# Layer-norm DMAs moved from ScalarE's queue to GpSimd's, with other buffers, copy priorities and filler positions at the end of a dilated attention

## Chip, cores and metric

One core of one Trainium2 chip. The metric is the device time of one execution in microseconds (us), the median of the runs shown. Engines: PE (TensorE), with PEld its weight loads, DVE (VectorE), ACT (ScalarE), POOL (GpSimd) and SP (SyncE, which here only issues DMAs). A name with q (ACTq, SPq) is an engine's instruction queue.

## What is computed

Two encoder layers on x of 512 tokens by 1024 features, all in float32. Each has three sub-layers, and each sub-layer ends in a layer norm over 1024 features:

```
x = layer_norm(ALPHA * x + h, ln_g[i, 0], ln_b[i, 0])                                  # h: token mixer
x = layer_norm(ALPHA * x + memory_cross_attention(...), ln_g[i, 1], ln_b[i, 1])
x = layer_norm(ALPHA * x + conv_glu(...), ln_g[i, 2], ln_b[i, 2])
```

The mixer of layer 0 is a differential attention with 8 heads. The mixer of layer 1 is a dilated window attention: 16 heads, three groups of (window, dilation), each with its own projections, merged by their softmax denominators.

## The kernel before

A float32 product is made of three PE passes over float32r halves (`mm3`, L239): high by high, high by low, low by high. Every weight is fetched from DRAM by SP as a 128x1024 tile `raw` (4 buffers) and split into `whi` (a cast on ACT, L219) and `wlo` (a subtraction on DVE, L220). So ACT and DVE feed PE, and DVE's subtraction frees the buffer into which SP fetches next.

**Order of the work.** PE's order is written by hand (`manual_schedule`): `weave` runs a main generator and, at each position that it yields, runs filler matmuls up to a matching share. The order of DVE, ACT, POOL and SP is made by the scheduler from the program's order and priorities; `tc.high_priority(offset=URGENT)` moves an instruction ahead. Each engine then runs its own list strictly in order, so an instruction that waits holds up all behind it, a DMA issue too.

**The dilated attention** (`dil_attention`) has 16 steps, a step being a pair of heads p and a half v of the queries. `scores(p, v)` puts four score tiles S into PSUM (4 buffers); for each, DVE adds the bias and takes the row extreme into a tile `u` (L730), and ACT takes the exponential in place (L732). `u` has 4 buffers, so the four tiles of a step can only be written once the four of the step before have been read. One step later `turn` transposes each of them on PE (L775) into one of two PSUM banks `ps_t`, and a copy to SBUF, `PT`, is made by DVE for tiles 0 and 2 and by ACT for 1 and 3 (L777). `values` (L790) multiplies by the value tiles; its result takes the same two banks. After v = 1 the two partial results `O` are scaled by `F` (L800 to L802) and split into the input of the output projection, `o1h` and `o1l`. `F` comes through `factors` (L745 to L769): small DMAs issued by POOL to DRAM and back.

The fillers are the projections of the next pair of heads and, for the last steps, `on_.early(0)`: the output projection of query block 0, as far as it goes without the last heads. `late` is the same for block 1 (12 units of one `mm3`, 648 by the planner's cost); `take(late, t)` runs units of it until their costs exceed t. In the last step (i = n = 16) there are no scores left: 3 units run at its head, 3 before `values`, the rest after the loop.

**The end of a sub-layer** (`OutNorm.finish`, L357) opens a pool of rows in memory that the attention has left (or in tiles of the ConvGLU). It loads gamma and beta broadcast to 128 partitions (`gb`, L368) and the four residual blocks (`xs`, L373), 512 KB each, by ACT's queue. While PE works through the four query blocks, `norm` (L418) does for each: two accumulating adds on DVE (L422, from PSUM), the mean (L425), the square on ACT (L426), two products (L429), a power -0.5 on POOL (L431), two more products (L434), and after each of the latter a 256 KB DMA of half the block to DRAM (L435), by ACT's queue. `turn` transposes the rows on PE for the next sub-layer (L440). Between, PE runs `mem_keys` (after a mixer): key projections of the memory tokens into two PSUM banks, which ACT and DVE empty into `kv` (L219, L220).

Of the kernel before, what the change touches and what calls it, by code (L numbers as in the profile page):

```python
# [9 lines left out]
F32 = mybir.dt.float32  # L10
# [6 lines left out]
D = 1024  # L17
# [131 lines left out]
def encoder(ctx: ExitStack, tc: tile.TileContext, wall, xin, lam, subln, conv, lngb, tabf, tabd, eye, out):  # L149
# [101 lines left out]
    def sl(k, n=128):  # L251
        return slice(k * n, k * n + n)
# [28 lines left out]
    def take(gen, t):  # L281
        while t > 0:
            d = next(gen, None)
            if d is None:
                break
            t -= d
# [40 lines left out]
    class OutNorm:  # L327
# [29 lines left out]
        def finish(self, banks, first, res, last, turns, lead_in, rows=None, then=(), norm=NORM):  # L357

            ln, nu = self.ln, self.nk // 2
            with ExitStack() as c:
                if rows is None:
                    tp = c.enter_context(tc.tile_pool(name=f"tail{ln}", bufs=1, reuse_waits="tile"))
                    rows = lambda n, dt=F32: tp.tile([128, D], dt, name=f"row{n}")
                gb = [rows(n) for n in range(2)]
                for n in range(2):
                    nc.scalar.dma_start(gb[n], bass.AP(lngb.tensor, lngb.offset + (ln * 2 + n) * D,  # L368
                                                       [[0, 128], [1, D]]))
                xs = [rows(2 + q) for q in range(4)]  # L370
                tmp, sq = rows(6), rows(7, BF16)
                for q in range(4):
                    nc.scalar.dma_start(xs[q], res[sl(q), :])  # L373
                ynext, act = None, None
                if not last:
                    ynext = dram.tile([SEQ, D], F32, name=f"y{ln}")
                    act = new_act(f"x{ln}")

                def left(u, q, hf):
                    if (u, q, hf) not in self.done:  # L380
                        run(self.part(u, q, hf))

                look["n"] = 0
                for us, qs in first:
                    for u in us:
                        self.load(*u)
                    for q in qs:
                        if q not in self.acc:
                            self.acc[q] = banks(q)
                    for u in us:  # L390
                        for q in qs:
                            left(u[0], q, u[1])
                ready = 0.0
                for q in range(4):
                    for us, qs in then if q == 2 else ():
                        for n in qs:
                            for u in us:
                                self.load(*u)
                                left(u[0], n, u[1])
                        pump(len(queue) + 1)  # L400
                    for n, hf in ((q, 0), (1, 0), (q, 1)) if q == 0 else ((q, 0), (q, 1)):
                        for u in range(nu):
                            self.load(u, hf)
                            left(u, n, hf)
                    self.norm(q, xs[q], gb, out if last else ynext, tmp, sq)
                    pump(PUMP[q])
                    if not last:
                        ready = max(ready, pe["now"]) + norm
                        for n in range(2):
                            due.append((ready + 700 * n,  # L410
                                        lambda q=q, n=n, x=xs[q], where=places(turns(q)):
                                        self.turn(q, n, x, act, where(n))))
                look["n"] = LOOK
                led = lead_in(act)
                flush()
                return act, ynext, led

        def norm(self, q, xs, gb, dst, tmp, sq):  # L418
            sm = st.tile([128, 6], F32, name="sm6", tag="sm6")
            for hf in range(2):  # L420
                f = sl(hf, 512)
                nc.vector.scalar_tensor_tensor(xs[:, f], xs[:, f], ALPHA, self.acc[q][hf],  # L422
                                               op0=ALU.mult, op1=ALU.add, accum_out=sm[:, hf:hf + 1])
            nmu, ss, ve, rs = (sm[:, n:n + 1] for n in range(2, 6))
            nc.vector.tensor_scalar(nmu, sm[:, 0:1], sm[:, 1:2], -1.0 / D, op0=ALU.add, op1=ALU.mult)  # L425
            nc.scalar.activation(sq, xs, AF.Square, bias=nmu, accum_out=ss)  # L426
            for n in range(2):
                f = sl(n, 512)
                nc.vector.scalar_tensor_tensor(tmp[:, f], xs[:, f], nmu, gb[0][:, f], op0=ALU.add, op1=ALU.mult)  # L429
            nc.vector.tensor_scalar(ve, ss, 1.0 / D, EPS, op0=ALU.mult, op1=ALU.add)  # L430
            nc.gpsimd.tensor_tensor(rs, ve, mhalf[:, 0:1], op=ALU.pow)  # L431
            for n in range(2):
                f = sl(n, 512)
                nc.vector.scalar_tensor_tensor(xs[:, f], tmp[:, f], rs, gb[1][:, f], op0=ALU.mult, op1=ALU.add)  # L434
                nc.scalar.dma_start(dst[sl(q), f], xs[:, f])  # L435

        def turn(self, q, n, xs, act, ps):
            tps = ps.rearrange("p (a b) -> p a b", b=128)
# [212 lines left out]
    def dil_attention(act, oT, pools, vp, ap, on_, led):  # L651
# [57 lines left out]
        def scores(p, v):  # L709
            (q0, k0, q1, k1, q2, k2) = qk[p]  # L710
            if v == 0:
                st0[p] = ap.tile([128, 4, 4], F32, tag="st0", name="st0")
                st12[p] = ap.tile([128, 4, 4], F32, tag="st12", name="st12")
            bs = 2 * v, 2 * v + 1
            Ss = {(b, c): psS.tile([128, 512], F32, tag="s", name="S") for b in bs for c in range(2)}
            for b in bs:
                for q_, k_, f in ((q0, keys(k0, b), slice(0, 256)), (q1, k1[:, b, :], slice(256, 384)),
                                  (q2, k2[:, b, :], slice(384, 512))):
                    for c in range(2):
                        h = sl(c, 64)  # L720
                        nc.tensor.matmul(Ss[b, c][:, f], q_[h, b, :], k_[h], start=True, stop=True)  # L721
            us = []
            for (b, c), S in Ss.items():
                u = ap.tile([128, 512], F32, tag="u", name="u", bufs=4)
                slope = 2.0 ** (-(2 * p + c + 1) / 2.0)
                for n, s in enumerate((st0[p], st12[p])):
                    f = sl(n, 256)
                    t = tab[:, 512:768] if n else tab[:, sl(b // 3, 256)]
                    m = s[:, b, 2 * c:2 * c + 1]
                    nc.vector.tensor_tensor_reduce(out=u[:, f], in0=S[:, f], in1=t, scale=-slope,  # L730
                                                   scalar=3.0e38, op0=ALU.add, op1=ALU.min, accum_out=m)
                    nc.scalar.activation(u[:, f], u[:, f], AF.Exp, bias=m, scale=-1.0,  # L732
                                         accum_out=s[:, b, 2 * c + 1:2 * c + 2])
                us.append(u)
            if v == 1:
                O[p] = [ap.tile([128, 512], F32, tag=f"O{n}", name="O", bufs=1) for n in range(2)], factors(p)
            return us
# [34 lines left out]
        def turn(u, n):  # L772
            tp = bank(pt, "t").rearrange("p (a b) -> p a b", b=128)
            for k in range(4):
                nc.tensor.transpose(tp[:, k, :], u[:, sl(k)], ident)  # L775
            PT = ap.tile([128, 4, 128], F32, tag="PT", name="PT", bufs=4)
            (nc.scalar.copy if n % 2 else nc.vector.tensor_copy)(PT, tp)  # L777
            return PT

        def values(p, v, PTs):  # L780
# [29 lines left out]
        def main():  # L810
            n = 2 * NP
            us = {}
            for i in range(n + 1):
                seg, step = (i // 2, 1 / 2.0) if i < n - 2 else (NP - 1, 1 / 3.0)
                pos = seg + (i - 2 * seg) * step
                yield pos
                if i < n:
                    us[i] = scores(i // 2, i % 2)
                else:
                    take(late, 1300)  # L820
                if i > 0:
                    PTs = []
                    for k in range(4):
                        yield pos + TURNS[k] * step
                        PTs.append(turn(us[i - 1][k], k))
                    yield pos + VALUES * step
                    if i == n:
                        take(late, 1300)
                    values((i - 1) // 2, (i - 1) % 2, PTs)
# [238 lines left out]
```

## Time and profile before

| | us |
|---|---|
| median of 3 runs | 1895.67 |
| the 3 runs | 1895.67, 1891.98, 1896.01 |
| the profiled execution, its own time | 1891.74 |
| span of its trace, first to last instruction | 1889.9 |
| PE busy in the span | 1864.7 |
| mean granted clock of PE | 0.997 |

The span leaves out 1.84 us of the execution. PE is busy for nearly all of it, so what can be saved without taking matmuls away is the little time in which PE waits, and the time in which it runs at a lower clock.

### The profile page before, as it was taken

The numbers are of one execution on the slowest core, as the hardware profiler recorded it, in microseconds if no ns is written. First come the engines' busy times: TensorE is split into PE (matmuls) and PEld (weight loads), VectorE is DVE, ScalarE is ACT, GpSimd is POOL, SyncE is SP. The second block draws the span as 40 slices with busy tenths as digits, with TensorE's granted clock in tenths as the row PEclk, the third lists the DMA queues.
The fourth block names the chain that finished last, engine by engine and source line by source line (L and its number), as shares of the span: only waits on it lengthen the run. The fifth ranks groups of instructions, "written<-read, shape, count | busy, mean of one in ns | idle before, by whom it ended". The sixth has DMA issues, their size and how long they took to land.

```text
span 1889.9 us, 25002 instructions
## 1 busy us (share of the span) xinstructions
PE 1864.7 (99%) x9896; PEld 1575.4 (83%) x9896; DVE 951.2 (50%) x1761; ACT 762.7 (40%) x1372; POOL 79.7 (4%) x116
## 2 busy tenths in 40 slices
PE   9999989999999999999999999999999999999998
PEld 7777778889888888899898898987888898888886
DVE  5678675547444432443444344445845564444324
ACT  5577644425333321234434344344544343333211
POOL 0011110000000000000000000001100000000000
PEclk9999999999999999999999999999999999999999
DMA  6121165234333234343223232231752343233241
GB/s 238 49 75 45 35 223 187 70 112 157 91 100 100 91 99 144 103 141 101 91 68 94 86 92 88 71 98 47 253 170 67 112 157 100 91 100 100 90 144 45
DMA packets 61573, 204.35 MB, mean 108 GB/s; under 512 B 8080, under 2 KB 8720, under 8 KB 61456
## 3 DMA queue, kind: packets, MB, share of 16 engines
q1 hardware_dynamic: 46080, 165.89, 27.6%
q10 hardware_dynamic: 12816, 32.47, 4.7%
q0 software_dynamic: 2560, 4.39, 1.0%
q8 instruction: 78, 1.28, 0.3%
q14 instruction: 39, 0.32, 0.1%
HBM read 190.01 MB, written 12.71 MB: 107 GB/s over the span
## 4 chain that ended last, share of the span: by engine, by line
PE 89%; DVE 4%; ACT 2%; DMA 2%; issue 1%; POOL 1%; DVEq 0%; POOLq 0%; SPq 0%; ACTq 0%
PE ps_a L240 16%; PE ps_a L241 16%; PE ps_a L242 16%; PE ps_o L240 7%; PE ps_o L241 7%; PE ps_o L242 7%; PE ps_s L242 2%; PE ps_s L241 2%; PE ps_s L240 2%; PE ps_t L240 2%; PE ps_t L242 2%; PE ps_t L241 2%; PE S L721 2%; PE ps_t L790 2%; PE ps_t L775 1%; ACT u L571 1%
## 5 line engine op out<-in xcount | busy, mean ns | idle before, releaser
L220 DVE TENSOR_TENSOR wlo<-raw,whi 128x1024 fp32r<-128x1024 f32 (+1 forms) x309 | 377.0, 1220 | 480.8 <-ACT whi L219 476.2
L219 ACT CAST whi<-raw 128x1024 fp32r<-128x1024 f32 (+1 forms) x309 | 323.9, 1049 | 583.7 <-PE ps_a L241 266.5
L240 PE MATMUL ps_a<-x2h,whi 128*128 128x512 f32 (+1 forms) x384 | 149.3, 389 | 0.0
L242 PE MATMUL ps_a<-x2h,wlo 128*128 128x512 f32 (+1 forms) x384 | 146.5, 382 | 0.0
L241 PE MATMUL ps_a<-x2l,whi 128*128 128x512 f32 (+1 forms) x384 | 146.3, 381 | 0.0
L240 PE MATMUL ps_a<-whi,x2h 128*128 128x512 f32 (+1 forms) x256 | 88.8, 347 | 0.0
L241 PE MATMUL ps_a<-wlo,x2h 128*128 128x512 f32 (+1 forms) x256 | 87.2, 341 | 0.0
L242 PE MATMUL ps_a<-whi,x2l 128*128 128x512 f32 (+1 forms) x256 | 87.2, 341 | 0.0
L242 PEld LDWEIGHTS ps_a<-x2h,wlo 128*128 128x128 f32 x384 | 72.2, 188 | 14.1
L240 PEld LDWEIGHTS ps_a<-x2h,whi 128*128 128x128 f32 x384 | 72.3, 188 | 13.9
L241 PEld LDWEIGHTS ps_a<-x2l,whi 128*128 128x128 f32 x384 | 72.3, 188 | 12.8
L732 ACT ACTIVATE u<-u,st 128x256 f32<-128x256 f32 x128 | 63.6, 498 | 38.2 <-DVE st L730 38.2
L240 PE MATMUL ps_o<-x4h,whi 128*128 128x512 f32 (+1 forms) x192 | 71.6, 373 | 0.0
L240 PE MATMUL ps_o<-x1h,whi 128*128 128x512 f32 (+1 forms) x192 | 71.6, 373 | 0.0
L241 PE MATMUL ps_a<-x1l,whi 128*128 128x512 f32 (+1 forms) x192 | 71.3, 371 | 0.0
L241 PE MATMUL ps_a<-x4l,whi 128*128 128x512 f32 (+1 forms) x192 | 71.3, 371 | 0.0
L240 PE MATMUL ps_a<-x1h,whi 128*128 128x512 f32 (+1 forms) x192 | 71.3, 371 | 0.0
L240 PE MATMUL ps_a<-x4h,whi 128*128 128x512 f32 (+1 forms) x192 | 71.3, 371 | 0.0
L242 PE MATMUL ps_a<-x1h,wlo 128*128 128x512 f32 (+1 forms) x192 | 71.3, 371 | 0.0
L242 PE MATMUL ps_a<-x4h,wlo 128*128 128x512 f32 (+1 forms) x192 | 71.3, 371 | 0.0
L242 PE MATMUL ps_o<-x1h,wlo 128*128 128x512 f32 (+1 forms) x192 | 71.3, 371 | 0.0
L242 PE MATMUL ps_o<-x4h,wlo 128*128 128x512 f32 (+1 forms) x192 | 71.3, 371 | 0.0
(420 smaller groups left out, 4453.6 us busy)
## 6 DMA issues: line engine op xcount, KB each, us to landing
raw<-in_wall_dram SPq DMA_DIRECT2D x314, 512.0 KB, 3.5
y<-row ACTq DMA_DIRECT2D x40, 256.0 KB, 2.5
row<-y ACTq DMA_DIRECT2D x20, 512.0 KB, 4.8
row<-in_lngb_dram ACTq DMA_DIRECT2D x12, 512.0 KB, 4.7
F<-fd POOLq DMA_DIRECT2D x16, 256.0 KB, 4.2
row<-in_x_dram ACTq DMA_DIRECT2D x4, 512.0 KB, 8.2
out_dram<-row ACTq DMA_DIRECT2D x8, 256.0 KB, 2.1
raw<-in_wall_dram ACTq DMA_DIRECT2D x2, 256.0 KB, 4.2
```

Of the source, the lines that this page charges most:

```text
L219: nc.scalar.copy(hi, ps)
L220: nc.vector.tensor_tensor(lo, ps, hi.bitcast(F32), op=ALU.subtract)
L240: nc.tensor.matmul(ps, ah, bh, start=start, stop=False)
L241: nc.tensor.matmul(ps, ah, bl, start=False, stop=False)
L242: nc.tensor.matmul(ps, al, bh, start=False, stop=stop)
L571: nc.scalar.activation(u, u, AF.Exp, bias=m, scale=-1.0, accum_out=sm[:, c:c + 1])
L721: nc.tensor.matmul(Ss[b, c][:, f], q_[h, b, :], k_[h], start=True, stop=True)
L732: nc.scalar.activation(u[:, f], u[:, f], AF.Exp, bias=m, scale=-1.0, accum_out=s[:, b, 2 * c + 1:2 * c + 2])
L775: nc.tensor.transpose(tp[:, k, :], u[:, sl(k)], ident)
L790: nc.tensor.matmul(o[sl(c, 64), sl(2 * (n // 2) + x)], V[:, :64], PTs[2 * x + c][:, n, :], start=n % 2 == 0, stop=n % 2 == 1)
```

## The change

The loads of gamma, beta and the residual and the stores of the normed rows are issued by GpSimd; the stores of the last norm, which write the output, are issued by SP. The four `u` tiles of the last but one step, (p, v) = (7, 0), are taken from the buffers of the value tiles `V1` (8 buffers, of which four belong to heads that are done by then). The copies of the transposes get URGENT priority. In the last step `late` no longer runs at the head: 3 units run before the first transpose, 5 before the third, and 3 before `values` as before.

```diff
@@ finish
                 for n in range(2):
-                    nc.scalar.dma_start(gb[n], bass.AP(lngb.tensor, lngb.offset + (ln * 2 + n) * D,
+                    nc.gpsimd.dma_start(gb[n], bass.AP(lngb.tensor, lngb.offset + (ln * 2 + n) * D,
                                                        [[0, 128], [1, D]]))
                 xs = [rows(2 + q) for q in range(4)]
                 tmp, sq = rows(6), rows(7, BF16)
                 for q in range(4):
-                    nc.scalar.dma_start(xs[q], res[sl(q), :])
+                    nc.gpsimd.dma_start(xs[q], res[sl(q), :])
@@ norm
-                nc.scalar.dma_start(dst[sl(q), f], xs[:, f])
+                (nc.sync if dst is out else nc.gpsimd).dma_start(dst[sl(q), f], xs[:, f])
@@ dil_attention: scores
             for (b, c), S in Ss.items():
-                u = ap.tile([128, 512], F32, tag="u", name="u", bufs=4)
+                if (p, v) == (NP - 1, 0):
+                    u = ap.tile([128, 512], F32, tag="V1", name="u", bufs=8)
+                else:
+                    u = ap.tile([128, 512], F32, tag="u", name="u", bufs=4)
@@ dil_attention: turn
-            (nc.scalar.copy if n % 2 else nc.vector.tensor_copy)(PT, tp)
+            with tc.high_priority(offset=URGENT):
+                (nc.scalar.copy if n % 2 else nc.vector.tensor_copy)(PT, tp)
@@ dil_attention: main
                 if i < n:
                     us[i] = scores(i // 2, i % 2)
-                else:
-                    take(late, 1300)
                 if i > 0:
                     PTs = []
                     for k in range(4):
                         yield pos + TURNS[k] * step
+                        if i == n and k % 2 == 0:
+                            take(late, 2600 if k else 1300)
                         PTs.append(turn(us[i - 1][k], k))
```

## Rows read from the trace of the kernel before

**Rows 1.** From the page: the span, and the chain of work that ended last by engine.
```profile
span 1889.9 us, 25002 instructions
...
PE 89%; DVE 4%; ACT 2%; DMA 2%; issue 1%; POOL 1%; DVEq 0%; POOLq 0%; SPq 0%; ACTq 0%
```
**Rows 2.** The waits of PE over the whole span: what waited, for whom, us in total, times, the longest.
```profile
PE ps_a L240 <- DVE kv L220: 7.2, 3, 4.9
PE ps_t L775 <- DVE PT L777: 1.9, 2, 1.4
```
**Rows 3.** Busy time of each engine in four stretches of 8 us at the end of the dilated attention (us, then busy us and instructions by engine, granted PE clock, DMA share, GB/s).
```profile
1278.00:1286.00 8.00, 8.00 (x75) 6.67 (x74) 4.87 (x17) 4.18 (x12) 1.64 (x3) 1.00 0.34 97
1286.00:1294.00 8.00, 6.43 (x60) 5.03 (x58) 4.51 (x21) 5.09 (x18) 1.83 (x3) 1.00 0.40 107
1294.00:1302.00 8.00, 6.34 (x53) 4.98 (x50) 5.66 (x17) 3.69 (x13) 0.79 (x1) 1.00 0.00 0
1302.00:1310.00 8.00, 7.13 (x61) 5.88 (x60) 2.22 (x8) 2.83 (x10) 1.64 (x3) 1.00 0.04 4
```
**Rows 4.** The timeline in those stretches: start, duration, engine and line, and in brackets the idle time of the engine before it and what ended it.
```profile
1298.57 0.42 DVE L730 CUSTOM_DVE_ANT_0 u<-S,tabd 128x256 f32<-128x256 f32 x1
...
1300.78 0.63 PE L775 MATMUL ps_t<-ident,u 128*128 128x128 f32 x4 [1.43 <-DVE PT L777]
...
1303.86 1.97 PE L790 MATMUL ps_t<-PT,V 128*64 128x128 f32 x32 [0.87 <-DVE PT L777]
```
**Rows 5.** The timeline behind them: the last factors' DMA, the first filler of PE behind the last `values`, the scaling by F, and the split of the last heads' result.
```profile
1304.34 0.54 POOL L747 DMA_DIRECT2D sd<-st  x1
...
1316.86 0.50 PE L240 MATMUL S<-whi,o1h 128*128 128x512 f32 x1
...
1319.59 0.69 DVE L800 TENSOR_TENSOR O<-O,F 128x512 f32<-128x512 f32 x1 [1.54 <-DMA F<-fd]
...
1322.35 0.69 DVE L220 TENSOR_TENSOR o1l<-O,o1h 128x512 fp32r<-128x512 f32 x1 [0.74 <-ACT o1h L219]
```
**Rows 6.** The timeline at the first norm (layer 0, after the mixer): ACT's casts and its DMA issues, and DVE's adds of the first two blocks.
```profile
236.97 0.82 ACTq L368 DMA_DIRECT2D row<-in_lngb_dram  x2
...
239.74 1.05 ACT L219 CAST whi<-raw 128x1024 fp32r<-128x1024 f32 x1 [2.19 <-PE ps_o L242]
239.80 0.33 ACTq L373 DMA_DIRECT2D row<-in_x_dram  x1
...
242.47 1.39 ACTq L373 DMA_DIRECT2D row<-in_x_dram  x3
...
247.15 0.08 DVE L422 DVE_READ_ACCUMULATOR row<-row,ps_a 128x1 f32 x1
...
249.82 0.69 DVE L422 SCALAR_TENSOR_TENSOR row<-row,ps_s 128x512 f32<-128x512 f32 x1 [2.58 <-DMA row<-in_x_dram]
```
**Rows 7.** The chain of work that ended last, at the first norm, in order of time: start, duration, what (DMA pieces run from issue to landing).
```profile
242.47 7.33 DMA row<-in_x_dram
...
260.25 5.83 DMA raw<-in_wall_dram
```
**Rows 8.** PE's timeline where the first norm holds it up, and two stretches (4 us there and 2 us at the fourth norm) with busy time and granted clock; the second answer shows PE alone.
```profile
276.51 0.58 PE L240 MATMUL ps_a<-mh,whi 128*128 128x256 f32 x1 [4.87 <-DVE kv L220]
276.89 0.42 PE L241 MATMUL ps_a<-ml,whi 128*128 128x256 f32 x1
...
281.16 0.29 PE L240 MATMUL ps_a<-mh,whi 128*128 128x256 f32 x1
...
276.00:280.00 4.00, 3.49 (x16) 3.49 (x17) 4.00 (x10) 2.44 (x4) 0.49 (x1) 0.50 0.49 153
...
1356.00:1358.00 2.00, 0.26 (x2) 1.00 0.87 326
```
**Rows 9.** The timeline at the fourth norm (layer 1, after the mixer).
```profile
1326.87 1.34 ACTq L373 DMA_DIRECT2D row<-y  x3
...
1332.34 0.69 DVE L422 SCALAR_TENSOR_TENSOR row<-row,S 128x512 f32<-128x512 f32 x1 [0.86 <-DMA row<-y]
...
1357.74 0.39 PE L240 MATMUL ps_a<-mh,whi 128*128 128x256 f32 x1 [1.85 <-DVE kv L220]
```
**Rows 10.** By source line, two DMAs of 256 KB: issues and their duration on the queue (ns, least, median, most), then us from issue to landing. First F's loads, issued by POOL, then the norms' stores, issued by ACT.
```profile
L769 POOL DMA_DIRECT2D F<-fd x16: 532/536/538, 923.0 to 1315.6; - x16
...
DMA to landing us min/median/max: 3.4/4.2/6.6
...
L435 ACTq DMA_DIRECT2D y<-row x40: 326/326/333, 254.1 to 1525.9; - x40
...
DMA to landing us min/median/max: 2.0/2.1/5.1
```
**Rows 11.** The power on POOL: all of its instances by source line (ns), and two rows of the first norm's timeline.
```profile
L431 POOL TENSOR_TENSOR sm<-sm,mhalf x24: 547/548/1460, 252.7 to 1883.9; 128x1 f32<-128x1 f32 x24
...
253.29 1.41 DVE L434 SCALAR_TENSOR_TENSOR row<-row,sm,row 128x512 f32<-128x512 f32 x2 [0.54 <-POOL sm L431]
...
256.18 1.46 POOL L431 TENSOR_TENSOR sm<-sm,mhalf 128x1 f32<-128x1 f32 x1 [2.92 <-DVE sm L430]
```
**Rows 12.** The timeline behind the third norm: its last stores, and the first write into memory that the rows had.
```profile
811.68 0.99 ACTq L435 DMA_DIRECT2D y<-row  x2
...
820.56 0.53 ACT L674 ACTIVATE f<-ps_a 64x448 f32<-64x448 f32 x1
```

## The prediction

> **What bounds the kernel now.** I read the page first: PE is on 89% of the chain that ended last [rows 1], so only PE's waits and its slow clock can be saved. Next come the waits of PE over the whole span: two releasers carry nearly all, DVE's evacuation of `kv` (7.2 us in 3 times) and the copies `PT` at L777 [rows 2]. Then the windows at these places.
>
> At the end of the dilated attention PE idles 1.57, 1.66 and 0.87 us in three stretches of 8 us, 4.1 us together, while in the stretch before them it is busy for all 8.00 [rows 3]. The cause is DVE's order: in the last steps there is little filler between scores and transposes, the exponentials' tiles `u` are free only after the transposes of the step before, so DVE's L730 comes late (1298.57) and the copy that PE needs stands behind four of them; PE waits 1.43 us for a bank and 0.87 us before `values` [rows 4].
>
> At the first norm PE idles 4.87 us and then runs at a granted clock of 0.50, the lower level of 1.2 GHz, up to 281.16 [rows 8]. The chain leads back through a weight fetch to a residual load issued at 242.47 [rows 7]. The reader is to see why it left so late: ACT's list has gamma, beta at 236.97, then a cast that waits 2.19 us for PE, then the first block at 239.80, and the other three just behind the next cast [rows 6]. The two `gb` issues needed no cast, the residual issues follow one within 0.06 us, so ACT's order held them. DVE, done with block 0 at 247.23, then stands 2.58 us for block 1 [rows 6].
>
> At the fourth norm the same pattern costs less: DVE waits 0.86 us for a row, PE 1.85 us for `kv` [rows 9].
>
> **The change part by part.** All is summed against the profiled execution's 1891.74 us.
>
> *Tail of the dilated attention* (`u` in V1 buffers, URGENT copies, `late` between the transposes). No instruction is added or removed. With (7, 0) in other buffers, its L730 can start when its scores are in PSUM, and (7, 1) then finds `u` read one step earlier; DVE is busy only 4.5 to 5.7 us of these 8 us stretches [rows 3], so the copies come in time. Of 4.1 us I keep 0.2 for the copy that `values` needs: **-3.9 us**; bounds 0 (DVE's order stays as it is) and -4.1. In the steady steps before, URGENT changes nothing for PE: busy 8.00 of 8 us, the waits hidden by filler [rows 3]. Five units of `late` move from behind `values` to ahead of it, so the last heads' result is needed 5 x 0.648 = 3.2 us sooner after `values`. It was ready at 1323.04, 6.2 us after the first filler behind `values` at 1316.86, of which 1.54 us was a wait for F [rows 5]. From that filler PE still has 1 unit of `late`, 8 units for blocks 2 and 3 and one for head pair 6 before it reads pair 7: 10 x 0.648 = 6.5 us by the planner's cost of a unit. F goes out some 4 us sooner because the last exponentials do, so 6.2 - 1.5 = 4.7 us against 6.5: cost nothing; if F were late, its wait would come back against that 1.8 us.
>
> *Loads by POOL, first norm.* Twelve gamma and beta and 24 residual loads leave ACT's queue in the whole kernel. POOL's issue takes 0.536 us by F's rows [rows 10]; six from 237.0 put block 1, the fourth, at 238.6 and done issuing at 239.1, 3.4 us before 242.47. F's landing is 4.2 against 2.1 us for the same size by ACT [rows 10], so 2.1 us of it may be lost; also the loads then share the DMA engines from the start. Block 1 then lands between 246.5 and 249, against 249.80; DVE could use it at 247.2. I take **2.5 us** for DVE, near the 2.58 it waited: the better end, since all six are then issued before ACT issued its second residual load. Bounds 0 and 2.6. From there to `kv` the chain is DVE, a fetch that DVE's subtraction releases (5.83 us) and DVE again [rows 7], so it moves with DVE: PE's wait falls from 4.87 to 2.4 us: **-2.5 us**. The clock: an idle of 1.85 us left it at 1.00, one of 4.87 ended in 0.50 [rows 8, 9]. 2.4 is nearest to 1.85, so I take it as unbroken. From 276.89 to 281.16 PE ran at half rate, 4.27 us of which half is lost: **-2.1 us**; bounds 0 and -2.1.
>
> *Fourth norm.* PE's frame comes 4 us sooner, but the memory of the rows is partly that of `O` and `F`, held until 1323.04 [rows 5]; in the new order `values` ends at 1316.86 - 4.1 + 3.2 = 1316.0, and this at 1320.7. If all six loads wait for it, block 1 is issued at 1320.7 + 4 x 0.54 = 1322.9, which is 1327.0 in the old frame, as late as the 1326.87 of before [rows 9], and lands up to 2.1 us later; if only two wait, it gains the 0.86. Bounds -0.9 and +2.3; I take **0**, between them, since the issue stays where it was.
>
> *Stores by POOL.* 40 of 256 KB, 0.54 us each, plus 8 on SP, whose list is empty by then. POOL's power for a block stands behind the two stores of the block before: those wait for L434, which ends at 254.70 [rows 11], so POOL is free by 255.8, and the power began at 256.18. Cover 0.4 us; without it DVE's L434 starts that much later, at four blocks at most 1 us a norm. Landing 2.1 us later has cover too: rows' memory is first written at 820.56, 8 us after the stores at 811.68 to 812.67 [rows 12]. ACT loses 84 issues of 0.33 us and waits for L434; PE waited for ACT hardly anywhere. Cost nothing; other norms nothing, as PE waits there for a few tenths.
>
> **Sum**: -3.9 - 2.5 - 2.1 + 0 = -8.5, so 1883.2 for an execution like the profiled one. One run of three agrees with that one (1891.98), two are 4 us above, and the median is one of those; no row says what parts them, and the weak place may be this norm's clock. I set 2 us for it, half the gap: **1885.3**.
>
> **A rule against the rule of thumb here.** The rows say that ACT's order, not its issue time, delays the loads. The Trainium skill (DMA: Bandwidth & Descriptors, Issuing engines are not separate DMA queues) says that issuing from several engines saves only the sequencer's time. By that the norms would give nothing; it is the second case below.
>
> **Rivals.**
> 1. *Only the tail gains.* The loads leave sooner but land no sooner, because F's 4.2 us and six loads at once eat the 3.4 us. For: the doubled landing [rows 10]. Against: 3.4 is more than 2.1. 1891.74 - 3.9 = 1887.8, or 1891.8 from the median.
> 2. *The fourth norm takes part of the tail's gain back*: loads held by `O`, then slower, +2.3 us there, and its wait of 4.2 us drops the clock, +2: 1883.2 + 4.3 = 1887.5, 1891.4 from the median.
> 3. *The tail's waits stay*, the change not doing what it says: the scheduler's list still has L730 ahead of the copy. 1891.74 - 4.6 = 1887.1. For: the list is fixed in advance by estimated times. Against: the buffers free it whatever the order.
> 4. *Slower: POOL's loads land late at both norms.* Place: block 1 at the first and fourth norm. POOL and DVE disturb each other: the power takes 0.55 us alone and 1.46 beside DVE's subtraction [rows 11]. If a 512 KB load takes twice F's longest 6.6 us, 13.2: at the first norm it lands at 252.3, 2.5 us later than before; at the fourth, in the new frame, at 1336.1 against 1328.2 (1332.3 less 4.1), 7.9 us late, and 2.1 us of clock: -3.9 + 2.5 + 7.9 + 2.1 = +8.6, so 1900.3. It decides from a landing of about 10 us: the first norm keeps 0.7, the fourth loses 4.8 and 2.1. Against: POOL's own issue never stretched (532 to 538 ns) [rows 10].
>
> The Trainium skill (SBUF — State Buffer, SBUF: two separate sides) says that GpSimd cannot write its DMA descriptors while certain DVE operations hold the shared port, and advises ACT or SP instead. The rows of the power agree on the lock; the unvarying issue time does not show it for DMAs.
>
> **How the numbers follow.** A measurement of this kernel tells about 0.2%, 3.8 us, from no change. Forecast 0.50, all faster; rival 1 0.20 (0.12 faster, 0.08 same, as its two frames differ); rival 2 0.12 (0.09, 0.03); rival 3 0.08 (0.05, 0.03); rival 4 0.10 slower. Faster 0.76, same 0.14, slower 0.10. The low end is all of it: 1891.74 - 4.1 - 4.87 - 2.1 - 0.9 = 1879.8, less 1.8 of spread, 1878. The high end is rival 1 or 2 with the bounds and the median's frame: 1894.5. Outside is rival 4.
>
> **What would show it.** Right: PE's waits for `PT` gone at the tail and three stretches near 8.0 of 8; residual loads on POOL issued within 4 us of each other at the first norm; DVE's wait for a row there under 0.5 us; PE's wait for `kv` near 2.4 us with the clock at 1.00; the fourth norm near 2 us. Wrong: DVE waits of 2 us or more for a row, a clock of 0.50 at either norm, powers on POOL starting behind stores, or a PE wait for `o1h` after the dilated attention.

## The result and the profile after

After: 1883.18 us, the median of 5 runs (1882.82 to 1884.51). Before, in the same group: 1894.5 (1891.98 to 1896.01). The ratio is 0.9943, with a 95% interval of 0.9929 to 0.9957: 11 us less. The profiled executions are nearer to each other, 1891.74 and 1884.51: the one of before is faster than all five of its group, and the one of after is the slowest of its five.

In the program after, the lines from L725 on have moved by 3 or 4 (L730 is L733, L755 is L758, L777 is L781, L790 is L794, L800 is L804). The page has PE on 91% of the chain where it was on 89% [rows 1]:

```profile
span 1882.7 us, 25064 instructions
...
PE 91%; DVE 3%; ACT 3%; issue 1%; DMA 1%; POOL 1%; POOLq 0%; DVEq 0%; ACTq 0%
```

PE's waits over the span: the wait for `kv` at the norms [rows 2] is gone, and the one for `PT` is still there:

```profile
PE ps_t L778 <- DVE PT L781: 2.2, 2, 2.0
PE ps_a L240 <- ACT whi L219: 1.2, 2, 0.8
PE ps_a L169 <- DVE warm L166: 1.2, 1, 1.2
PE ps_a L241 <- DVE wlo L220: 1.2, 2, 0.8
```

**First norm.** The timeline of POOL, then that of DVE, which answers to [rows 6]. POOL issues all six loads by 241.3; DVE adds blocks 0 and 1 with no wait for a row (2.58 us before):

```profile
237.61 1.22 POOL L368 DMA_DIRECT2D row<-in_lngb_dram  x2
239.20 2.09 POOL L373 DMA_DIRECT2D row<-in_x_dram  x4 [0.37 <-issue]
```
```profile
246.40 0.68 DVE L422 SCALAR_TENSOR_TENSOR row<-row,ps_a 128x512 f32<-128x512 f32 x1
...
247.03 0.69 DVE L422 SCALAR_TENSOR_TENSOR row<-row,ps_s 128x512 f32<-128x512 f32 x1
...
272.78 0.42 DVE L220 TENSOR_TENSOR kv<-ps_a,kv 128x256 fp32r<-128x256 f32 x1
```

PE then has no row with a wait where it waited 4.87 us [rows 8]; the windows there (us, PE's busy time and instructions, granted clock, DMA share, GB/s) are full at a clock of 1.00:

```profile
272.00:274.00 2.00, 2.00 (x18) 1.00 0.69 217
274.00:276.00 2.00, 2.00 (x19) 1.00 0.75 252
276.00:278.00 2.00, 2.00 (x19) 1.00 0.84 254
```

**End of the dilated attention.** The windows that answer to [rows 3], and two short ones for PE alone:

```profile
1278.00:1286.00 8.00, 5.85 (x47) 4.62 (x47) 5.32 (x29) 4.84 (x18) 1.14 (x2) 1.00 0.25 70
1286.00:1294.00 8.00, 8.00 (x73) 6.69 (x72) 3.19 (x12) 3.07 (x12) 1.16 (x3) 0.79 0.28 68
1294.00:1302.00 8.00, 7.58 (x62) 5.98 (x61) 4.79 (x14) 4.32 (x14) 1.87 (x3) 1.00 0.04 3
1302.00:1310.00 8.00, 7.70 (x43) 6.27 (x42) 2.15 (x11) 0.69 (x2) 0.61 (x2) 1.00 0.01 1
```
```profile
1286.00:1288.00 2.00, 2.00 (x11) 0.59 0.10 4
1288.00:1290.00 2.00, 2.00 (x24) 0.55 0.27 78
```

One stretch is full where one was before, but at a clock of 0.79: behind an idle time of 1.95 us PE runs 4 us near its lower level (0.50, 1.2 GHz). The longest wait has moved to one step earlier, and the timeline of DVE, then that of PE, shows its new cause [rows 4]:

```profile
1278.99 0.43 DVE L733 CUSTOM_DVE_ANT_0 u<-S,tabd 128x256 f32<-128x256 f32 x1
...
1281.57 0.17 DVE L758 TENSOR_TENSOR w<-x,st 128x8 f32<-128x8 f32 x1 [2.14 <-DMA x<-sd]
...
1284.20 0.69 DVE L781 COPY PT<-ps_t 128x512 f32<-128x512 f32 x1
```
```profile
1284.94 0.66 PE L778 MATMUL ps_t<-ident,u 128*128 128x128 f32 x4 [1.95 <-DVE PT L781]
...
1295.97 1.09 PE L778 MATMUL ps_t<-ident,u 128*128 128x128 f32 x8 [0.23 <-ACT PT L781]
...
1308.83 1.09 PE L778 MATMUL ps_t<-ident,u 128*128 128x128 f32 x8 [0.30 <-DVE PT L781]
...
1321.30 0.50 PE L240 MATMUL ps_a<-whi,o1h 128*128 128x512 f32 x1 [0.40 <-ACT whi L219]
1322.56 0.50 PE L241 MATMUL ps_a<-wlo,o1h 128*128 128x512 f32 x1 [0.76 <-DVE wlo L220]
...
1325.96 0.50 PE L241 MATMUL ps_a<-wlo,o1h 128*128 128x512 f32 x1 [0.41 <-DVE wlo L220]
```

DVE's L733 does start early, as the buffers allow. But the list then has an operation on the shares of head pair 6 (L758), which stands 2.14 us for a DMA, ahead of seven L733 and the copy. In the kernel before, the same operation had no wait:

```profile
1284.59 0.16 DVE L755 TENSOR_TENSOR w<-x,st 128x8 f32<-128x8 f32 x1
```

**Fourth norm.** The last three rows above are 1.57 us of new waits; those for `kv` (1.85 us [rows 9] and 0.46) are gone. DVE and POOL show why the new ones came; the first row answers to the wait of 1.54 us for F and the next to the last sd of [rows 5]:

```profile
1317.56 0.69 DVE L804 TENSOR_TENSOR O<-O,F 128x512 f32<-128x512 f32 x1 [1.88 <-DMA F<-fd]
```
```profile
1298.28 0.54 POOL L750 DMA_DIRECT2D sd<-st  x1
1305.67 0.58 POOL L752 DMA_DIRECT2D x<-sd  x1 [6.86 <-issue]
...
1321.32 2.09 POOL L373 DMA_DIRECT2D row<-y  x4 [6.28 <-DVE o1l L220]
```

The last sd is issued 6.1 us earlier than before, 5.5 of which PE's own work is ahead by since the first norm. But x<-sd goes out 7.39 us after it (3.72 before), so F is later against PE's work, and the casts for PE stand behind it. Of these 3.67 us, 1.5 are a longer landing of sd (4.69 against 3.16) and 2.1 an idle time of POOL that the last section shows.

**What every profile lost, by place.** For each run, PE's idle time plus what the clock took (busy time times one minus the granted clock), summed over windows of 2 us at the first norm, the end of the dilated attention and the fourth norm, and the time from the last store's issue to the end of the span:

```
                          first norm  dilated end  fourth norm  end    median us (ratio)
before                    4.9 + 2.3   4.2          2.3          3.9    1891.4 to 1894.5
the whole change          0           2.9 + 1.7    1.6          3.1    1883.18 (0.9943)
the whole change, again   0           3.1          1.7          3.1    1882.60 (0.9950)
1 norms' DMAs             0           6.3          0.3          3.1    1884.35 (0.9960)
2 dilated part            2.3 + 1.6   2.1          4.9 + 2.2    3.9    1891.21 (0.9994)
3 loads only              0           4.2          0.3          6.9    1886.62 (0.9970)
4 memory casts early      1.6         4.1          1.4          4.0    1886.93 (0.9968)
5 stores only             1.3         4.4          2.6          3.4    1887.38 (0.9976)
6 shares later            0           1.6          0.2          3.1    1879.52 (0.9935)
6 shares later, again     0           1.0          0.2          3.1    1879.19 (0.9932)
7 y stores on ACT         0           1.1          0.3          6.9    1883.67 (0.9955)
8 norms' DMAs and V1      0           3.3 + 1.7    0.1          3.1    1882.22 (0.9950)
9 mem casts held          0.3         3.4          1.7          3.1    1883.59 (0.9956)
10 norms, urgent, late    0           2.2          1.8          3.2    1882.52 (0.9953)
```

From before to after the four columns give -7.2, +0.4, -0.7 and -0.8: -8.3 us. The two spans differ by only 7.2, mostly because PE's start took 1.7 us longer in the profiled execution after (ACT's first cast o0h at the norm is at 238.68 against 236.97). Between 5.7 and 9.9 us its first products took 0.6 to 0.8 us each there, where before they took 0.4 to 0.5, though the windows show a clock of 1.00 for both.

### The profile page after: what moved, and what is told of

Read it like the earlier page. It is cut to its first block, busy times and chain, and to the rows that moved or that the text cites. A ratio compares the mean times of both kernels' runs of the same rounds, so it can differ in the third digit from the quotient of the medians.

```text
span 1882.7 us, 25064 instructions
## 1 busy us (share of the span) xinstructions
PE 1865.8 (99%) x9896; PEld 1575.8 (84%) x9896; DVE 951.2 (51%) x1761; ACT 764.6 (41%) x1372; POOL 119.2 (6%) x192
## 4 chain that ended last, share of the span: by engine, by line
PE 91%; DVE 3%; ACT 3%; issue 1%; DMA 1%; POOL 1%; POOLq 0%; DVEq 0%; ACTq 0%
PE ps_a L240 17%; PE ps_a L241 16%; PE ps_a L242 16%; PE ps_o L240 7%; PE ps_o L241 7%; PE ps_o L242 7%; PE ps_s L242 2%; PE ps_s L241 2%; PE ps_s L240 2%; PE ps_t L242 2%; PE ps_t L240 2%; PE ps_t L241 2%; PE S L721 1%; PE ps_t L794 1%; PE ps_t L778 1%
## 5 line engine op out<-in xcount | busy, mean ns | idle before, releaser
L241 PEld LDWEIGHTS ps_a<-x2l,whi 128*128 128x128 f32 x384 | 72.3, 188 | 12.8
```

The lines of the kernel that those rows point to most:

```text
L241: nc.tensor.matmul(ps, ah, bl, start=False, stop=False)
```

## The experiments

Three groups of four, each on one chip beside runs of the kernel before (medians 1892.42, 1892.4 and 1891.41).

**1. All of the norms' DMAs moved, the dilated attention as before.**

> All DMAs of the norms leave ACT's queue, the dilated attention is left as it was. Theory: this part carries the whole gain. At the first norm the wait of PE for kv (4.87 us) and the stretch at half clock (2.1 us) go, at the fourth norm the waits for kv (1.85 and 0.46 us): about -9 us, 0.995 of before; and the three PE waits for PT at the end of the dilated attention stay at 4.1 us. Rival (the forecast's sum): the first norm gives 4.6 us and the fourth nothing, -4.6 us, 0.9976.

Measured: 1884.35 us, 0.996 (0.9947 to 0.9972), -8.1 us. The theory's 9 is a little high because a third wait appeared at the end of the dilated attention:

```profile
1306.47 1.09 PE L775 MATMUL ps_t<-ident,u 128*128 128x128 f32 x8 [2.25 <-DVE PT L777]
```

It belongs to x<-sd, 5.86 us after the last sd. So this part carries most of the gain, and costs some 2.2 us elsewhere.

**2. The dilated attention alone.**

> Only the dilated attention is changed (buffers of V1, urgent copies, fillers between the transposes); the norms' DMAs stay on ACT. Theory: PE's waits only change their releaser. With u free, DVE's list meets the factors of head pair 6, which wait about 2 us for the DMA x<-sd ahead of L733 and the copy; PE waits about 2 us there, and its clock may fall behind it. Gain under 1.5 us, 0.9993 to 1.0005 of before; first norm unchanged (kv 4.87 us, clock 0.50). Rival (the forecast): -3.9 us, 0.998, windows of the tail near 8.0 of 8 us.

Measured: 1891.21 us, 0.9994 (0.9985 to 1.0003). The forecast's -3.9 is out. The end of the dilated attention does fall from 4.2 to 2.1 us, and what is left is a wait for ACT's copy (1.73 us), not one for the shares; so the theory is right in the sum and not in the place. This wait, too, goes back to an instruction of DVE that stands for a DMA, now for pair 6's F. An L733 stands behind it, and ACT's exponential, ahead of the copy in ACT's list, waits for that L733. DVE's row, then ACT's:

```profile
1293.93 0.69 DVE L804 TENSOR_TENSOR O<-O,F 128x512 f32<-128x512 f32 x1 [1.41 <-DMA F<-fd]
```
```profile
1295.66 0.51 ACT L735 ACTIVATE u<-u,st 128x256 f32<-128x256 f32 x1 [2.07 <-DVE st L733]
```

What the tail gave, this profile loses at the fourth norm, where the loads are still on ACT: DVE stands for a row, and PE for `kv` as long as at the first norm of before. DVE's row, then PE's:

```profile
1328.22 0.69 DVE L422 SCALAR_TENSOR_TENSOR row<-row,ps_a 128x512 f32<-128x512 f32 x1 [4.65 <-DMA row<-y]
```
```profile
1355.40 0.58 PE L240 MATMUL ps_a<-mh,whi 128*128 128x256 f32 x1 [4.87 <-DVE kv L220]
```

**3. Loads only** (`gb` and `xs` on POOL, `dst` on ACT).

> Only the 36 loads of the norms (gamma, beta, residual) go to POOL; the 48 stores stay on ACT. Theory: ACT's list gets the two casts mh ahead of the norm's statistics as soon as the loads are out of it, so this has the whole gain of the norms' DMAs: within 1.5 us of the run with both. Rival: the stores matter too, since they stand in ACT's list until DVE's L434 has written the row, ahead of casts: 3 us or more slower than the run with both.

Measured: 1886.62 us, 0.997 (0.9957 to 0.9982), 2.3 us slower than with both: between theory and rival. At the norms nothing is left to gain (0 and 0.3 us); the difference stands at the end, where the span goes on for 6.9 us behind the last store instead of 3.1, in time that no row fills.

**4. The memory casts early, all DMAs as before.**

```diff
@@ mem_load
-            evac(raw, mt[0]..., mt[1]...)
+            with tc.high_priority(offset=40):
+                evac(raw, mt[0]..., mt[1]...)
```

> All DMAs stay on ACT and where they were in its list, the dilated attention too; only the casts of the memory tokens (mh on ACT, ml on DVE) get a priority that puts them right behind the last residual load, ahead of the norm's statistics. Theory: the order of these casts held the raw buffers, and with them the weights for kv: PE's wait for kv at the first norm falls under 1 us with the clock at 1.00, -6 to -9 us, 0.995 to 0.997, though block 1 lands as late as before (DVE waits about 2.5 us for it). Rival (the forecast's mechanism): the late landing of block 1 is the cause; then kv waits over 3.5 us as before and the time changes by under 2 us.

Measured: 1886.93 us, 0.9968 (0.9955 to 0.998); the longest wait for `kv` is 1.19 us. That seemed to make the order of the casts the cause. But block 1 had not landed as late as before: DVE waited 1.35 us for it instead of 2.58. The run alone does not decide.

**5. Stores only** (`dst` on POOL and SP, loads on ACT).

> Only the 48 stores of the norms leave ACT (40 to POOL, the last 8 to SP); loads on ACT and the dilated attention as before. Theory: the stores by themselves are worth nothing at the norms: PE's wait for kv at the first and fourth norm stays (2 to 5 us each); the store on SP ends the kernel 0.8 us sooner after the last store (3.1 instead of 3.9 us); and the DMA x<-sd of the last head pair goes out 5.5 us or more after the last sd (3.7 before), so PE has a third wait for PT of about 2 us at the end of the dilated attention. Sum about +1 us: 0.9995 to 1.0015 of before. Rival: the stores are what parts the run with both (1884.35) from the one with loads only (1886.62): -2.3 us, 0.9988, by less blocking of ACT at the norms.

Measured: 1887.38 us, 0.9976 (0.9966 to 0.9986), -5 us. Both numbers missed. x<-sd went out 3.95 us after the last sd, so the stores alone do not delay it; the first norm lost 1.3 us, the tail 4.4. Part of that is again a row that came sooner (DVE waits 0.59 us), part that ACT's list no longer stands for L434 ahead of casts (DVE's waits for `whi` there 4.39 us, 5.85 before). One profile does not part the two; the table behind the experiments does so by an estimate.

**6. The whole change, with the shares of pair 6 written later**, so that the operation that waits for x has more L733 ahead of it. Run twice.

```diff
@@ scores
-                O[p] = [...], factors(p)
+                f = factors(p)              # issues sd and x<-sd, returns the rest
+                O[p] = [[...], f if p == NP - 2 else f()]
@@ main, behind the transposes of a step
+                    if (i - 1) % 2 and callable(O[(i - 1) // 2][1]):
+                        O[(i - 1) // 2][1] = O[(i - 1) // 2][1]()
```

> The whole change, and in it the arithmetic on the shares of head pair 6 (the small DVE operations behind the DMA x<-sd) is written behind the transposes of the next step, so that DVE's list has four L733 more ahead of the operation that waits for x. Theory: that operation is what holds the PT copy in the whole change (PE 1.95 us, then clock 0.57): PE's wait falls to about 0.9 us, the clock stays at 1.00, 2 to 3 us less than the whole change: 0.992 to 0.993 of before. Rival: another thing is as late (the transposes' banks, ACT's copy); then PE's wait stays at 1.5 us or more, and the time is that of the whole change, 0.9943.

> The whole change with the shares of pair 6 written behind the next transposes, once more, beside the whole change on one chip. Theory: 2 to 4.5 us less than the whole change in the same group (the tail's loss 1.5 instead of 4.2 us, the fourth norm's 0 to 1.6). Rival: the two are within 1 us, and what parted them (1883.18 and 1879.52) was the group.

Measured: 1879.52 us, 0.9935 (0.9921 to 0.9948); again, beside the whole change: 1879.19, 0.9932 (0.992 to 0.9945), against 1882.60. So 3.4 us less, the fastest of all. In the table the tail and the fourth norm together fall from 4.8 to 1.2 us. PE waits before `values` alone in the second of these runs, and its windows are nearly full at a clock of 1.00. First PE's timeline, then the windows:

```profile
1285.30 1.97 PE L800 MATMUL ps_t<-PT,V 128*64 128x128 f32 x32 [0.34 <-DVE PT L787]
...
1295.88 1.09 PE L800 MATMUL ps_t<-PT,V 128*64 128x128 f32 x16 [0.48 <-DVE PT L787]
```
```profile
1278.00:1286.00 8.00, 7.56 (x64) 6.06 (x66) 5.92 (x29) 5.59 (x20) 0.35 (x2) 1.00 0.22 71
1286.00:1294.00 8.00, 7.91 (x76) 6.57 (x72) 4.84 (x20) 5.30 (x20) 3.63 (x6) 1.00 0.28 67
```

The last sd is issued at 1293.24 instead of 1296.83, so F is in time although x<-sd is late here too.

**7. The same with the 40 stores of y on ACT.**

> Like the run with the shares later, but the 40 stores of y stay on ACT; loads on POOL, the 8 stores of the result on SP. Theory: what delays x<-sd of the last pair on POOL by some 2 us is the stores on POOL, so here it goes out under 4.5 us after the last sd, F is in time and PE has no waits for whi and wlo at the fourth norm (1.6 us in the whole change); the end takes 3.1 us after the last store as with SP, not 6.9 us as with loads only: 1880 to 1882 us, 0.991 to 0.9935 of before, the fastest of all. Rival: the stores on ACT cost by themselves what parted the loads-only run (1886.62) from both (1884.35): then it is 2 us slower than the run with the shares later.

Measured: 1883.67 us, 0.9955 (0.9942 to 0.9967): the rival's side, 4 us slower. x<-sd went out 2.19 us after sd and the fourth norm lost 0.3 us, as the theory had it; but the end took 6.9 us again, though SP issued the last stores. So the long end does not belong to the engine that stores the result.

**8. The norms' DMAs and the V1 buffers.**

> All DMAs of the norms as in the change, and of the dilated attention only the buffers of V1 (no urgent copies, fillers behind the transposes as before). Theory: the buffers alone remove PE's waits of 1.42, 0.87 and 0.86 us and bring the one for the shares of pair 6 (about 2 us); the third wait for PT (2.25 us, since x<-sd is late and no filler stands between the last transposes) stays: 6.3 us at the end of the dilated attention become 4 to 4.5, 1882.3 us, 0.995 of before or a little less. Rival: without the urgent copies the buffers bring nothing, the tail keeps 6.3 us and the time 1884.4.

Measured: 1882.22 us, 0.995 (0.9937 to 0.9962), 2.1 us less than run 1: the theory's size, in part by chance. PE's long wait was one of 2.12 us for DVE's copy, but the third one, which the theory kept, was gone, and the clock, which it did not count, took 1.7 us.

**9. The whole change once more, and with the memory casts held back.** In the second, `mh` waits for the power of a block.

```diff
@@ mem_load
+            if len(held) < 8:
+                nc.vector.tensor_copy(mt[0][:, 4 * n, 0:1], held[-1])    # held: rs of each norm
```

> The whole change once more, beside the kernels of this group. Theory: the two waits that its profile shows in the tail (1.95 us for the PT copy behind the shares of pair 6, with the clock at 0.57 after it, and 1.6 us for whi and wlo behind a late F) belong to the program, so they are there again; 0.994 to 0.995 of before. Rival: they belonged to that one execution (its time was the longest of five); then the profile shows under 3 us of both together and the time is that of the run with the shares later, 0.9935 or less.

> The whole change, but at the first norm the two casts mh must wait until the power of block 1 is there (one value of it is copied into the tile before the cast writes it), as late as they were in the kernel before, while the residual rows land as early as in the change. Theory: the casts hold the raw buffers and so the weights for kv: PE's wait for kv at the first norm is back with 3 us or more, 3 to 7 us above the whole change (0.996 to 0.998 of before). Rival (the forecast's mechanism): the early landing of the rows makes the gain; then PE waits under 1 us for kv and the time is within 1 us of the whole change.

Measured: 1882.60 us, 0.995 (0.9937 to 0.9962), with both losses there again (3.1 and 1.7 us), though the clock stayed up this time (waits of 1.27 and 1.34 us; in the second, DVE stands 1.02 us for pair 6's F, as in run 2). With the casts held: 1883.59 us, 0.9956 (0.9943 to 0.997), only 1 us more. The casts start at 258.16, later than in the kernel before (251.82 and 255.11), and PE still has no wait but 0.33 us. **So the gain does not need the casts early.** That the landing of the rows alone makes it is not shown: the stores are off ACT's list here too. ACT's cast, DVE's `kv`, PE's wait:

```profile
258.16 2.00 ACT L219 CAST mh<-raw 128x1024 fp32r<-128x1024 f32 x2 [1.67 <-DVE mh L457]
```
```profile
272.84 0.42 DVE L220 TENSOR_TENSOR kv<-ps_a,kv 128x256 fp32r<-128x256 f32 x1
```
```profile
283.43 0.39 PE L240 MATMUL ps_a<-mh,whi 128*128 128x256 f32 x1 [0.33 <-DVE kv L220]
```

**10. The norms' DMAs with the urgent copies and the fillers, without V1.**

> All DMAs of the norms as in the change, and of the dilated attention the urgent copies and the fillers between the last transposes, but u in its own four buffers. Theory: with the urgency DVE's list has each PT copy ahead of the four L730 that it stood behind, so the waits of 1.43 and 0.87 us mostly go without any new buffers, and the fillers cover the third (2.25 us): the tail falls from 6.3 to under 2.5 us, 1880 to 1882 us, 0.9945 or less of before. Rival: without free buffers L730 and the exponentials come late whatever the copies do, and the next transposes wait for those: the tail keeps over 4 us, 1884 us.

Measured: 1882.52 us, 0.9953 (0.994 to 0.9965), a little over the theory's 1880 to 1882. The tail lost 2.2 us instead of 6.3, so the urgent copies and the fillers together do it without new buffers; no run parts these two. The late F cost 1.8 us at the fourth norm.

## Why the prediction came out

The forecast was 1885.3 and faster (its terms add up to 1885.2); measured were 1883.18 and, in another group, 1882.60. The sum of the places, -8.3, is near the forecast's -8.5, but its terms are not: the tail brought 4.3 us less than forecast, the first norm 2.6, the fourth 0.7 and the end 0.8 us more. That these errors cancelled is luck.

**First norm: right mechanism, too small.** Counted from ACT's cast o0h, PE needs the bank that DVE's first `kv` frees 34.67 us later in all four kernels in which it waits (before: 276.51 - 4.87 - 236.97). When DVE gets there:

```
                         DVE waits for a row   for whi   DVE starts kv at   PE waits
before                   2.58                  5.85      +39.07             4.87
2 dilated part           0.22                  5.63      +36.49             2.28
4 memory casts early     1.35                  4.05      +35.40             1.19
5 stores only            0.59                  4.39      +35.07             0.87
the whole change         0                     2.71      +34.10             0
9 mem casts held         0                     4.05      +33.78             0
```

Run 2 has this norm's program unchanged; only the row landed 2.36 us sooner, DVE came 2.58 us sooner, and PE waited 2.28. That is the forecast's 2.5 and its 2.4 almost exactly, by chance in an unchanged program. PE's row in run 2:

```profile
274.35 0.56 PE L240 MATMUL ps_a<-mh,whi 128*128 128x256 f32 x1 [2.28 <-DVE kv L220]
```

It may also be what the runs of before scatter by (1888 to 1896 us, where those after lie within some 2 us): their mean granted clock falls with the time, from 0.999 to 0.996, as it would with such a wait, but only the profiled ones show where. The step that failed is "it moves with DVE": I let DVE's other waits stand, and they shrank too, `whi` by 3.1 us, POOL's power and PE's banks by 1.3. With the 2.58 for the row that is more than the 5.0 us by which `kv` comes sooner, since 1.5 us more work of DVE now stands ahead of it and another 0.4 us are new waits. So PE's wait went to nothing, not to 2.4.

What comes from the row and what from ACT's list can be estimated by taking the wait for the row off the start of `kv`. With the norms' DMAs on ACT in the old order 36.5 and 36.3 us are left (before, run 2), with the casts early 34.1 (run 4), with the stores off ACT's list 34.5 (run 5). So the row is worth up to 2.6 us here, and a shorter or better ordered list on ACT some 2 us more, for which the forecast had nothing ("cost nothing", "PE waited for ACT hardly anywhere"). Moving the loads alone is enough for both: in run 3 DVE starts `kv` at +32.95, and PE has no wait for it there. The margin of the whole change is thin: 34.10 and the 0.47 us to PE's start against 34.67. The clock's 2.1 us came back (2.3 by the windows), but the reason given for it did not hold: behind the 2.28 us of run 2 the clock did fall (1.6 us).

**Tail: wrong.** -3.9 was forecast, +0.4 and -1.1 measured in two profiles. Part of that is the price of POOL's DMAs: against run 1, whose tail lost 6.3 us, the dilated part brings 1.7 and 3.2 us at the tail and costs 1.3 and 1.4 at the fourth norm. "The copies come in time" failed, since the cover was read from DVE's busy share; DVE was idle, but standing for a DMA in the middle of its list. The buffers did what they should; the next thing late was the shares (in run 2 and the repeat also pair 6's F), which before had been hidden behind the later L730 (L755 had no wait in the old order). Run 6 moves that operation, which then has no wait either, and gets back 3.4 us, at the tail and the fourth norm together. The row is from its second profile:

```profile
1280.43 0.17 DVE L764 TENSOR_TENSOR w<-x,st 128x8 f32<-128x8 f32 x1
```

Rival 1 (only the tail gains) is the reverse of what came; rival 3 had the right result for the wrong reason: the list did hold L733 ahead of the copy, but what came late was L758. Of the forecast's own signs, the four residual loads on POOL within 4 us and DVE without a wait for a row came; the three full stretches did not.

**Fourth norm: 0 forecast, -0.7 measured**, made of -2.3 (no wait for `kv`) and +1.6 (late F). The forecast named the margin, 1.8 us for F, and POOL spent it: x<-sd was 3.7 us later against sd than before. F, forecast some 4 us sooner, was issued at 1313.41 instead of 1315.57; PE's work being 5.5 us ahead, that is 3.3 us later for PE. The loads were indeed held by `O`, as said: POOL stands 6.28 us for o1l. Yet DVE did not wait for a row. What rival 2 feared took place in run 2, with the loads on ACT: 4.9 + 2.2 us.

**Landing by POOL: the bounds were too wide.** The page's DMA issues after (count, KB each, median us to landing):

```profile
y<-row POOLq DMA_DIRECT2D x40, 256.0 KB, 2.9
row<-y POOLq DMA_DIRECT2D x20, 512.0 KB, 5.3
...
row<-in_x_dram POOLq DMA_DIRECT2D x4, 512.0 KB, 8.7
```

By ACT the same view of before has 2.5, 4.8 and 8.2: 0.4 to 0.5 us less, where the forecast allowed 2.1 from F's rows [rows 10]. (The 2.1 us that it had for ACT is a median over L435 that has the 8 stores of the output in it; the 40 stores of y alone have 2.5.) Over all profiles even this difference is not clear: the median of y<-row is 2.2 to 3.2 us in five by ACT and 2.7 to 2.9 in nine by POOL, that of row<-y 4.8 to 5.4 by either. Block 1's load leaves 4.5 us sooner at the first norm (1.0 us behind the cast o0h instead of 5.5). It lands 7.3 to 8.3 us behind that cast in the ten profiles with the loads on POOL, and with them on ACT at 12.8 in the profile of before, the latest of four, and at 10.5 to 11.6 in runs 2, 4 and 5. So about half of it or more is kept, and rival 4 had nothing to stand on. The stores cost nothing at the norms, as said, and off ACT's list they seem to help at the first (run 5); that the kernel ends 0.8 us sooner was not forecast.

The Trainium skill (DMA: Bandwidth & Descriptors, Issuing engines are not separate DMA queues) says that several issuing engines save only the sequencer's time. By that run 1 would have given next to nothing, and it gave 8.1 us: the landings bear the rule out, since they got no shorter, but what was saved was the place of the issues in an in-order list. (The prediction's "second case below" is its first rival, in which only the tail gains.) The Trainium skill (SBUF — State Buffer, SBUF: two separate sides) warns that POOL cannot write its descriptors while certain DVE operations hold the port that they share. No run here shows it: POOL's y stores took 539 to 594 ns to issue in the whole change, and no run tells which of DVE's operations hold that port.

## What to carry to other kernels

A DMA issue in a busy engine's list is late by what stands ahead of it, and it holds up what stands behind it. Move it to an idle queue, and count the consumer's whole path to the point where PE needs it, with every engine whose list gets shorter, not one wait. Before a wait is taken away, look down the waiting engine's own list for the next instruction that stands for a transfer: a busy share of 60% is no cover when that one stands ahead of the urgent one. An unchanged stage that differs between two profiles is an experiment for nothing: it prices one wait with all else equal.

## What was not expected of the hardware

**POOL stands 2.1 us longer at one place.** In all eight profiles with both the norms' loads and their y stores on POOL (the whole change, its repeat, runs 1, 8, 9 and 10 and both of run 6), pair 7's x<-sd is issued 2.7 us after the last sd has landed; in the six others, with one of the two kinds on POOL (runs 3, 5 and 7) or none (before, runs 2 and 4), 0.56. In the chain this is 2.62 us behind the landing's signal instead of 0.48. No row fills it; why is open. The chain after, then before:

```profile
1298.28 4.69 DMA sd<-st
1302.97 0.02 issue
1303.00 0.04 POOLq L752
1303.04 2.62 issue
```
```profile
1304.34 3.16 DMA sd<-st
1307.50 0.02 issue
1307.52 0.04 POOLq L749
1307.57 0.48 issue
```

**The end.** With loads on POOL and y stores on ACT the span runs 6.9 us past the last store's issue (runs 3 and 7), otherwise 3.1 to 4.0. The difference of 3 to 4 us is also open.

**The clock around 2 us of idle.** It fell behind waits of 1.95 (the whole change), 2.12 (run 8) and 2.28 us (run 2), and stayed at 1.00 behind 1.85 (before), 1.98 (run 5), 2.04 (run 10) and 2.25 us (run 1). An idle time of that size has no certain price here: nothing, or 1.6 to 1.7 us more.
